# Attention weighing in a one-core transformer step: values stationary in two column halves, four heads' probabilities moving, 1/den turned to feature-major

## The chip, the cores and the metric

The kernel runs on one core of a Trainium2 chip. The metric is the device time of one execution in microseconds (us). The core has TensorE (PE in the profile; its loads of the stationary operand are PEld), VectorE (DVE), ScalarE (ACT), GpSimd (POOL) and SyncE (SP); each works its own queue strictly in the order in which the program issues instructions, except that PE may load a stationary operand ahead. The whole program is written under a manual schedule: the order of the Python calls is the order in each queue.

## The reference, cut to what matters

Two trunk layers over 384 tokens (three tiles of 128: latent tiles 0 and 1, context tile 2) of 1024 features. Layer 0 is feed-forward, attention, feed-forward; layer 1 has a recurrent mixer in the middle. The change is in the attention:

```python
p = softmax_with_sink(s, sink)          # e / (sum(e) + exp(sink - m))
return jnp.einsum('bhgqk,bkhd->bqhgd', p, v)     # then @ w_attn_out
```

There are 16 query heads of 64 features and 4 key/value heads, so that four query heads (a quadruple) share one v. A latent tile of 128 queries sees three blocks of 128 keys, the context tile one block.

## The kernel before, in words

Weights stream from HBM through three raw buffers; each chunk of 512 KB is split by ACT (L195) and DVE (L196) into two parts of lower precision, and PE multiplies in three passes (`mm3`, L447 to L450). Beside this a planner spreads "units" of the modulation vectors (`pace`, L311; one unit is one DVE instruction on 1024 columns, L242 or L244, and every second unit needs a 512 KB load, L230) over calls of `pace` in each stage: `set_pace(n, calls)` says up to which unit and in how many calls.

The attention (`attention`, L745) has three stages: the projections to q, k and v (to L899); the core (L903 to L1028); and the output projection `project_out` (L465), whose stationary operand is `hT`, the feature-major attention output, in chunks of 128 features.

The core runs over 36 items: 16 heads of latent tile 0, four quadruples of context heads, 16 heads of latent tile 1. Iteration i of its loop issues, in this order:

- `expo(i + 1)` (L934, ACT): exponential of the scores with the sum along the row accumulated to `den`,
- `flip(i)` (L945): PE turns the probabilities, one 128x128 transpose for each key block (L950), and ACT copies them from PSUM to `pT` (L951),
- `score(i + 2)` (L913, PE): two matmuls (L920) and for latent items a mask matmul (L923), into one of three PSUM banks,
- `weigh(i - 1)` (L953, PE): for each head and key block one matmul (L960) with the turned probabilities stationary and the 64 columns of v moving; the result is token-major, 64 columns for each head,
- `top(i + 2)` and `shift(i + 2)` (L925, L929, DVE): row maximum and the bias for the exponential,
- `pace()`, and after items 3, 8, 13 and 18 a weight split.

When 8 heads are complete (a "half"), the events of `O_LAGS` (L34) are fired 0 to 5 iterations later: `o_prep` (exponential of the sink term), `o_norm` (DVE: add, reciprocal, and 512 columns times 1/den out of PSUM, L972 to L974), `o_turn` (four PE transposes to feature-major, L431), `o_hi` and `o_lo` (ACT and DVE write the two parts of `hT`, L435 and L440). The last half's events that lie behind the loop run inside `project_out` (`flush`, L1030). What an item hands on from engine to engine is PE score, DVE maximum and bias, ACT exponential, PE flip, ACT copy, PE weighing.

Of the kernel before, what the change touches and what calls it, by code (L numbers as in the profile page):

```python
# [33 lines left out]
O_LAGS = [(0, 1, 0), (2, 1, 1), (4, 0, 2), (4, 1, 3), (5, 1, 4)]  # L34
# [3 lines left out]
def hybrid_step_kernel(  # L38
# [103 lines left out]
    add_rows(w_attn_out[0])  # L142
# [23 lines left out]
    def w_dma():  # L166
        j = ws["dma"]
        if j < len(chunks):
            SP.dma_start(out=view_like(raw_of(j), chunks[j].shape), in_=chunks[j])
            ws["dma"] += 1  # L170
# [574 lines left out]
    def attention(pending, perm):  # L745
# [6 lines left out]
        set_pace(5.5, 9)  # L752
        aux[0] = None
        with ExitStack() as es:
# [9 lines left out]
            qs = pool.tile([P, NT, 16, 2, 64], F32, name="qs")  # L764
            k_sb = pool.tile([P, 4, 256], F32, name="k_sb")
            pb = [pool.tile([P, 512], F32, name=f"p{i}") for i in range(3)]
            pT = [pool.tile([P, 512], F32, name=f"pT{i}") for i in range(2)]
# [134 lines left out]
            oslot = {t: alloc() for t in range(2)}  # L902
# [42 lines left out]
            def flip(i):  # L945
# [5 lines left out]
                S.activation(out=pT[i % 2][:, 0:w * P], in_=tb[:, 0:w * P], func=AF.Copy)  # L951

            def weigh(i):  # L953
                t, h0, nh, n, k0 = shape(i)
                src = pT[i % 2]
                for a in range(nh):
                    h = h0 + a
                    for j in range(n):
                        o = (a * n + j) * P
# [5 lines left out]
            def o_prep(t, half):  # L965
                hs = slice(8 * half, 8 * half + 8)
# [3 lines left out]
            def o_norm(t, half, i):  # L970
                hs = slice(8 * half, 8 * half + 8)
                V.tensor_tensor(out=den[:, t, hs], in0=den[:, t, hs], in1=esk[:, hs], op=ALU.add)  # L972
                V.reciprocal(out=den[:, t, hs], in_=den[:, t, hs])
                V.tensor_tensor(  # L974
                    out=slots[oslot[i]][:, half * 512:half * 512 + 512].rearrange("p (h d) -> p h d", h=8),
                    in0=bank(6 + half).rearrange("p (h d) -> p h d", h=8),
                    in1=den[:, t, hs].unsqueeze(2).to_broadcast([P, 8, 64]), op=ALU.mult,
                )

            def o_turn(t, half, i):  # L980
                turn(slots[oslot[i]], t, (bank(5), bank(5)), (half,))
# [14 lines left out]
            events = {}  # L996
            nd = 0
            for i in range(n):
                t, h0, nh = items[i]
                if h0 + nh in (8, 16):  # L1000
                    half = (h0 + nh) // 8 - 1
                    for lag, step, fn in O_LAGS:
                        args = (t, half) if fn == 0 else (t, half, nd % 2)
                        events.setdefault((i + lag, step), []).append(((o_prep, o_norm, o_turn, o_hi, o_lo)[fn], args))
                    nd += half

# [4 lines left out]
            for i in range(n + 1):  # L1011
# [7 lines left out]
                if i > 0:  # L1019
                    weigh(i - 1)  # L1020
# [554 lines left out]
```

## Time and profile before

| | |
|---|---|
| median of 3 runs | 1604.59 us (1603.9 to 1604.62) |
| profiled execution | 1604.8 us, span 1603.0 us |
| PE busy in the span | 97% |
| core of the attention, first score to first matmul of the output projection | 383.21 to 447.20 us |

The span is the time from the first to the last instruction of the profiled execution; about 2 us of the execution lie around it. A busy PE is not PE at its peak, since matmuls overlap; how fast a stretch of PE work goes is read from the distance of starts.

### The profile page before, as it was taken

How to read it: one execution, taken by the hardware profiler on the slowest of the kernel's cores; microseconds unless marked ns; L12 is line 12 of the kernel's file. 1: busy time of each engine (PE TensorE's matmuls, PEld its weight loads, DVE VectorE, ACT ScalarE, POOL GpSimd, SP SyncE). 2: the span in 40 equal slices, each digit the busy share in tenths (PEclk: the TensorE clock that was granted, in tenths of full speed). 3: DMA queues.
4: the chain of work that ended last, by engine and by line, in shares of the span. 5: the costliest groups of instructions: out<-in, count | busy, mean ns of one | idle time of the engine just before them, and what ended most of it. 6: DMA issues, size and time to landing. Idle time of an engine off the chain costs nothing.

```text
span 1603.0 us, 22629 instructions
## 1 busy us (share of the span) xinstructions
PE 1556.7 (97%) x8846; PEld 1419.6 (89%) x8846; DVE 1050.1 (66%) x1385; ACT 659.4 (41%) x1123; POOL 162.4 (10%) x308
## 2 busy tenths in 40 slices
PE   6999999999999999999999999999999899999997
PEld 4899987887889999988999998889999789999885
DVE  3887788577747777885676788556665765444552
ACT  3432234465745223334423233456656444323341
POOL 1111111000010111120011111000000110000000
PEclk9999999999999999999999999999999999999999
DMA  8776767352125676674467667433233335544441
GB/s 304 248 248 213 223 216 238 100 158 69 64 93 172 210 216 217 200 241 140 135 209 215 206 211 247 147 119 109 85 112 88 110 108 167 158 147 130 148 141 40
DMA packets 164091, 264.50 MB, mean 165 GB/s; under 512 B 10432, under 2 KB 122144, under 8 KB 163984
## 3 DMA queue, kind: packets, MB, share of 16 engines
q1 hardware_dynamic: 140592, 187.27, 36.2%
q0 software_dynamic: 22864, 75.36, 15.4%
q8 instruction: 69, 1.13, 0.3%
q10 hardware_dynamic: 528, 0.43, 0.1%
q14 instruction: 38, 0.31, 0.1%
HBM read 260.01 MB, written 3.01 MB: 164 GB/s over the span
## 4 chain that ended last, share of the span: by engine, by line
PE 87%; DVE 6%; ACT 3%; issue 1%; DMA 1%; POOL 0%; DVEq 0%; POOLq 0%; ACTq 0%
PE pb L448 14%; PE pb L449 14%; PE pb L450 14%; PE pb L458 13%; PE pb L460 12%; PE pb L463 12%; DVE wl L196 1%; PE pb L960 1%; PE pb L269 1%; ACT wh L195 1%; PE pb L950 1%; PE pb L920 1%; DVE sig L1100 1%; DVE slot L244 1%; PE pb L1152 1%
## 5 line engine op out<-in xcount | busy, mean ns | idle before, releaser
L196 DVE TENSOR_TENSOR wl<-raw,wh 128x1024 fp32r<-128x1024 f32 x297 | 362.1, 1224 | 245.9 <-ACT wh L195 245.6
L195 ACT ACTIVATE wh<-raw 128x1024 fp32r<-128x1024 f32 x299 | 315.0, 1059 | 479.0 <-PE pb L463 319.4
L458 PE MATMUL pb<-hT,wh 128*128 128x384 f32 (+1 forms) x1248 | 411.1, 333 | 0.0
L460 PE MATMUL pb<-hT,wl 128*128 128x384 f32 (+1 forms) x1248 | 407.1, 330 | 0.0
L244 DVE SCALAR_TENSOR_TENSOR slot<-araw,sc,slot 128x1024 f32<-128x1024 f32 x224 | 282.3, 1279 | 0.0
L463 PE MATMUL pb<-hT,wh 128*128 128x384 f32 (+1 forms) x1248 | 260.4, 329 | 0.0
L458 PEld LDWEIGHTS pb<-hT,wh 128*128 128x128 f32 x1248 | 235.4, 189 | 6.2 <-issue 5.9
L460 PEld LDWEIGHTS pb<-hT,wl 128*128 128x128 f32 x1248 | 235.3, 189 | 0.2
L463 PEld LDWEIGHTS pb<-hT,wh 128*128 128x128 f32 x1248 | 216.4, 189 | 0.0
L448 PE MATMUL pb<-wh,gh 128*128 128x512 f32 x384 | 150.7, 393 | 0.2 <-DVE dump L279 0.2
L450 PE MATMUL pb<-wh,gl 128*128 128x512 f32 x384 | 149.5, 389 | 0.0
L449 PE MATMUL pb<-wl,gh 128*128 128x512 f32 x384 | 149.5, 389 | 0.0
L230 POOL DMA_DIRECT2D araw<-in_w_ada_dram x128 | 69.2, 541 | 689.6 <-DVE slot L244 574.2
L448 PE MATMUL pb<-hT,wh 128*128 128x384 f32 x352 | 119.6, 340 | 4.9 <-ACT hT L1451 4.9
L449 PE MATMUL pb<-hT,wh 128*128 128x384 f32 x352 | 119.0, 338 | 0.2 <-DVE hT L1455 0.2
L450 PE MATMUL pb<-hT,wl 128*128 128x384 f32 x352 | 118.4, 336 | 0.0
L448 PE MATMUL pb<-wh,hT 128*128 128x512 f32 (+1 forms) x258 | 93.7, 363 | 2.7 <-DVE slot L1310 1.9
L449 PE MATMUL pb<-wl,hT 128*128 128x512 f32 (+1 forms) x258 | 90.4, 350 | 0.8 <-DVE wl L196 0.8
L450 PE MATMUL pb<-wh,hT 128*128 128x512 f32 (+1 forms) x258 | 90.5, 351 | 0.0
L448 PEld LDWEIGHTS pb<-wh,gh 128*128 128x128 f32 x384 | 72.1, 188 | 19.4 <-issue 3.4
L450 PEld LDWEIGHTS pb<-wh,gl 128*128 128x128 f32 x384 | 72.1, 188 | 15.1
L449 PEld LDWEIGHTS pb<-wl,gh 128*128 128x128 f32 x384 | 72.1, 188 | 14.7
(236 smaller groups left out, 2069.1 us busy)
## 6 DMA issues: line engine op xcount, KB each, us to landing
raw<-in_w_ffn_in_dram SPq DMA_DIRECT2D x176, 512.0 KB, 4.5
araw<-in_w_ada_dram POOLq DMA_DIRECT2D x128, 512.0 KB, 4.5
raw<-in_w_ffn_out_dram SPq DMA_DIRECT2D x88, 512.0 KB, 4.0
raw<-in_w_rec_in_dram SPq DMA_DIRECT2D x40, 512.0 KB, 3.6
slot<-dsc POOLq DMA_DIRECT2D x24, 256.0 KB, 5.8
raw<-in_w_qkv_dram SPq DMA_DIRECT2D x12, 512.0 KB, 3.9
raw<-in_w_attn_out_dram SPq DMA_DIRECT2D x8, 512.0 KB, 3.3
raw<-in_w_rec_out_dram SPq DMA_DIRECT2D x8, 512.0 KB, 3.2
```

Of the source, the lines that this page charges most:

```text
L195: S.activation(out=h, in_=r, func=AF.Copy)
L196: ws["eng"].tensor_tensor(out=lo, in0=r, in1=h.bitcast(F32), op=ALU.subtract)
L230: G.dma_start(out=araw[j % NA], in_=w_ada[kd[0], (j % 8) * P:(j % 8 + 1) * P, acol(kd):acol(kd) + 1024])
L244: V.scalar_tensor_tensor(out=acc[v], in0=src, scalar=s_, in1=acc[v], op0=ALU.mult, op1=ALU.add)
L269: T.matmul(out=bank[32 * r:32 * r + 32, :], lhsT=ones, rhs=acc[v][:, 512 * h:512 * h + 512], start=True, stop=True, skip_group_check=True,)
L448: T.matmul(out=out, lhsT=a[0], rhs=b[0], start=start, stop=False, skip_group_check=True)
L449: T.matmul(out=out, lhsT=a[0], rhs=b[1], start=False, stop=False, skip_group_check=True)
L450: T.matmul(out=out, lhsT=a[1], rhs=b[0], start=False, stop=stop, skip_group_check=True)
L458: T.matmul(out=out, lhsT=a[0], rhs=b[0], start=start, stop=False, skip_group_check=True)
L460: T.matmul(out=out, lhsT=x, rhs=y, start=False, stop=False, skip_group_check=True)
L463: T.matmul(out=out, lhsT=x, rhs=y, start=False, stop=stop, skip_group_check=True)
L920: T.matmul(out=ps[:, a, :], lhsT=hv[:, t, h, :], rhs=rhs, start=s == 0, stop=s == 1 and t == 2, skip_group_check=True)
```

## The change: what it does

`weigh` no longer runs for each item. It runs once for each group of 8 heads (two quadruples, one iteration after the group's last item), with v stationary: 64 columns of v for one quadruple write the upper 64 partitions of a PSUM bank, those of the other quadruple the lower 64, and the moving operand is the four heads' turned probabilities, 4 x 128 = 512 columns. So 112 matmuls of 64 columns become 28 of 512, in groups of 6 (latent tiles) or 2 (context). The output is feature-major at once, with another order of the heads along the features, so the rows of `w_attn_out` are loaded in that order, two DMAs of 64 partitions for a chunk in place of one of 128.

Since the queries now lie along the columns, 1/den has to be feature-major too: DVE spreads it to `rd` (two copies of 256 columns), PE turns `rd` (four transposes), ACT copies the result to a slot, DVE multiplies it by the PSUM bank of the weighing, and ACT and DVE write the two parts of `hT` from the slot. `pT` now keeps the turned probabilities of whole groups, in the space of the finished `qs`; the copy out of PSUM goes to DVE for items with i % 5 in (1, 3), 14 of 36, and to ACT for the others. `pace()` leaves the core's loop; the 8 units that stood there are done in the first feed-forward stage (5.5 in place of 5 for its `set_pace`), and the projection stage does units 88 to 95 in place of 80 to 87.

```diff
-O_LAGS = [(0, 1, 0), (2, 1, 1), (4, 0, 2), (4, 1, 3), (5, 1, 4)]
...
-    add_rows(w_attn_out[0])
+    for k in range(KD):
+        heads = [8 * (k // 4) + 4 * q + k % 4 for q in range(2)]
+        chunks.append(tuple(w_attn_out[0, 64 * h:64 * h + 64, :] for h in heads))
...
+            if isinstance(c_, tuple):
+                for q in range(2):
+                    SP.dma_start(out=raw_of(j)[64 * q:64 * q + 64, :], in_=c_[q])
...
-        set_pace(5.5, 9)
+        set_pace(6, 9)
...
-                S.activation(out=pT[i % 2][:, 0:w * P], in_=tb[:, 0:w * P], func=AF.Copy)
-
-            def weigh(i):
...
+                if i % 5 in (1, 3):
+                    V.tensor_copy(out=dst, in_=src)
+                else:
+                    S.activation(out=dst, in_=src, func=AF.Copy)
+
+            def weigh(t, gp, c):
+                n, k0 = (3, 0) if t < 2 else (1, 3)
+                for j in range(n):
+                    for q in range(2):
                         T.matmul(
-                            out=bank(6 + h // 8)[:, (h % 8) * 64:(h % 8) * 64 + 64], lhsT=src[:, o:o + P],
-                            rhs=v_sb[:, k0 + j, (h // 4) * 64:(h // 4) * 64 + 64], start=j == 0, stop=j == n - 1,
+                            out=bank(6 + c % 2)[64 * q:64 * q + 64, :], lhsT=v_sb[:, k0 + j, (2 * gp + q) * 64:(2 * gp + q) * 64 + 64],
+                            rhs=pT[c % 2][:, 4 * q:4 * q + 4, j, :], start=j == 0, stop=j == n - 1, skip_group_check=True,
                         )
...
+            def o_den(t, gp, c):
+                hs = slice(8 * gp, 8 * gp + 8)
                 V.tensor_tensor(out=den[:, t, hs], in0=den[:, t, hs], in1=esk[:, hs], op=ALU.add)
                 V.reciprocal(out=den[:, t, hs], in_=den[:, t, hs])
+                dv = den[:, t, hs].rearrange("p (q a) -> p a q", q=2)
+                for q in range(2):
+                    V.tensor_copy(out=rd[:, :, q, :], in_=dv[:, :, q:q + 1].to_broadcast([P, 4, 64]))
+
+            def o_row(t, gp, c):
+                for a in range(4):
+                    T.transpose(bank(5)[:, a * P:(a + 1) * P], rd[:, a].rearrange("p q d -> p (q d)"), ident)
+
+            def o_mul(t, gp, c):
+                u = half_of(slots[oslot], c % 2)
+                S.activation(out=u, in_=bank(5), func=AF.Copy)
+                V.tensor_tensor(out=u, in0=u, in1=bank(6 + c % 2), op=ALU.mult)
...
-            set_pace(6, 30)
...
+                    for lag, step, fn in ((0, 1, o_prep), (1, 0, weigh), (1, 1, o_den), (2, 0, o_row), (2, 1, o_mul), (3, 0, o_hi), (3, 1, o_lo)):
...
-                if i > 0:
-                    weigh(i - 1)
...
-                pace()
...
-        done = ffn(0, 0, 5, None, [0, 1, 2, 3], between)
+        done = ffn(0, 0, 5.5, None, [0, 1, 2, 3], between)
```

Around the end of the first 8 heads PE's queue stands like this before the change (`p` are the probabilities, `cf` holds the identity for a transpose, `pb_70` and `pb_71` are the banks of the output; items 8 and 9 flipped, 10 and 11 scored, 7 and 8 weighed):

```order
L950 MATMUL pb_67<-cf,p_2398 128x128 x3
L920 MATMUL pb_65<-kT,hT 128x384 x2
L923 LDWEIGHTS eye
L923 MATMUL pb_65<-hide_2405,eye 128x128
L960 MATMUL pb_70<-v_sb,pT_2400 128x64 x3
L950 MATMUL pb_68<-cf,p_2396 128x128 x3
L920 MATMUL pb_66<-kT,hT 128x384 x2
L923 LDWEIGHTS eye
L923 MATMUL pb_66<-hide_2405,eye 128x128
L960 MATMUL pb_71<-v_sb,pT_2399 128x64 x3
```

and like this after it (`qs` is now the space of the turned probabilities, `rd` the spread 1/den):

```order
L958 MATMUL pb_67<-cf,p_2411 128x128 x3
L928 MATMUL pb_65<-kT,hT 128x384 x2
L931 LDWEIGHTS eye
L931 MATMUL pb_65<-hide_2416,eye 128x128
L970 MATMUL pb_70<-qs,v_sb 64x512 x6
L958 MATMUL pb_68<-cf,p_2409 128x128 x3
L928 MATMUL pb_66<-kT,hT 128x384 x2
L931 LDWEIGHTS eye
L931 MATMUL pb_66<-hide_2416,eye 128x128
L990 MATMUL pb_69<-cf,rd 128x128 x4
L958 MATMUL pb_67<-cf,p_2410 128x128 x3
```

The three matmuls of one item between each score and the next flip have become six for eight items, in one piece behind the score of item 10 and ahead of the flip of item 9.

DVE's queue at the same place before the change, from the maximum of item 10 on:

```order
L927 TENSOR_REDUCE mx_2402<-pb_65 128x1
L932 SCALAR_TENSOR_TENSOR nm<-mx_2402,nsink 128x1
L927 TENSOR_REDUCE mx_2403<-pb_66 128x1
L932 SCALAR_TENSOR_TENSOR nm<-mx_2403,nsink 128x1
L972 TENSOR_TENSOR den<-den,esk 128x8
L973 RECIPROCAL den<-den 128x8
L974 TENSOR_TENSOR slot_110<-pb_70,den 128x512
L927 TENSOR_REDUCE mx_2401<-pb_64 128x1
L932 SCALAR_TENSOR_TENSOR nm<-mx_2401,nsink 128x1
L927 TENSOR_REDUCE mx_2402<-pb_65 128x1
```

and after it, from just behind the maximum of item 10:

```order
L982 TENSOR_TENSOR den<-den,esk 128x8
L983 RECIPROCAL den<-den 128x8
L986 COPY rd<-den 128x4x64 x2
L935 TENSOR_REDUCE mx_2414<-pb_66 128x1
L940 SCALAR_TENSOR_TENSOR nm<-mx_2414,nsink 128x1
L995 TENSOR_TENSOR slot_110<-slot_110,pb_70 128x512
L935 TENSOR_REDUCE mx_2412<-pb_64 128x1
L940 SCALAR_TENSOR_TENSOR nm<-mx_2412,nsink 128x1
L1003 TENSOR_TENSOR hT<-slot_110,hT 128x512
L962 COPY qs<-pb_68 128x384
L935 TENSOR_REDUCE mx_2413<-pb_65 128x1
```

The multiplication (L995), the low part of `hT` (L1003) and a copy of turned probabilities (L962) now stand between the maxima of items 11, 12 and 13.

## Rows read from the trace of the kernel before

**Rows 1.** The page, its part on busy time, share of the span and instructions of each engine.

```profile
PE 1556.7 (97%) x8846; PEld 1419.6 (89%) x8846; DVE 1050.1 (66%) x1385; ACT 659.4 (41%) x1123; POOL 162.4 (10%) x308
```

**Rows 2.** Busy time of each engine in stretches (us from the span's start, length, busy and count of PE, PEld, DVE, ACT, POOL, then the granted TensorE clock as a share of full speed, DMA share, GB/s): ten us of the first feed-forward stage, then the attention's projections, core and output projection.

```profile
240.00:250.00 10.00, 10.00 (x45) 8.28 (x45) 8.90 (x10) 4.25 (x6) 1.06 (x2) 1.00 0.76 248
341.00:383.20 42.20, 39.51 (x208) 32.76 (x206) 31.29 (x50) 21.34 (x39) 2.12 (x4) 1.00 0.48 157
383.20:447.20 64.00, 60.33 (x484) 52.47 (x484) 45.91 (x110) 46.34 (x146) 2.12 (x4) 1.00 0.14 45
447.20:500.00 52.80, 51.55 (x298) 43.89 (x298) 29.98 (x46) 26.23 (x52) 9.35 (x19) 1.00 0.35 111
```

**Rows 3.** Who waited for whom in the core, 383.2 to 447.2 us: engine, tile and line, what it waited for, us in total, times, longest.

```profile
PE pb L950 <- ACT p L940: 3.4, 4, 1.4
PE pb L920 <- ACT hT L883: 0.6, 1, 0.6
...
DVE mx L927 <- PE pb L923: 11.8, 15, 2.6
...
ACT p L940 <- DVE nm L932: 11.9, 16, 1.8
```

**Rows 4.** Timeline of PE's loads of the stationary operand in one steady round of the core (start, length): flip, score, mask, weighing, next flip.

```profile
404.56 0.37 PEld L950 LDWEIGHTS pb<-cf,p 128*128 128x128 f32 x3
404.90 0.30 PEld L920 LDWEIGHTS pb<-kT,hT 128*128 128x128 f32 x2
405.36 0.10 PEld L923 LDWEIGHTS <-eye 128*128 128x128 bf16 x1 [0.16 <-issue]
405.37 0.76 PEld L960 LDWEIGHTS pb<-v_sb,pT 128*128 128x128 f32 x6
405.99 0.20 PEld L950 LDWEIGHTS pb<-cf,p 128*128 128x128 f32 x1
```

**Rows 5.** Timeline of all engines at the start of the core, where nothing is weighed yet: flip of item 0, then item 2 from its score to its flip.

```profile
385.58 0.31 PEld L950 LDWEIGHTS pb<-cf,p 128*128 128x128 f32 x3 [1.33 <-ACT p L940]
...
385.86 0.30 PEld L920 LDWEIGHTS pb<-kT,hT 128*128 128x128 f32 x2
...
386.59 0.56 DVE L927 TENSOR_REDUCE mx<-pb 128x1 f32<-128x384 f32 x1 [1.16 <-PE pb L923]
...
387.18 0.16 DVE L932 SCALAR_TENSOR_TENSOR nm<-mx,nsink 128x1 f32<-128x1 f32 x1
...
387.43 0.58 ACT L940 ACTIVATE p<-pb,nm 128x384 f32<-128x384 f32 x1 [0.78 <-DVE nm L932]
...
388.16 0.20 PEld L950 LDWEIGHTS pb<-cf,p 128*128 128x128 f32 x2 [0.33 <-ACT p L940]
```

**Rows 6.** Timeline of PE's loads: the flips of items 15 (last of tile 0), 20 (first of tile 1) and 35 (last), and the first load of the output projection.

```profile
407.83 0.26 PEld L950 LDWEIGHTS pb<-cf,p 128*128 128x128 f32 x2
...
419.82 0.31 PEld L950 LDWEIGHTS pb<-cf,p 128*128 128x128 f32 x3
...
445.35 0.31 PEld L950 LDWEIGHTS pb<-cf,p 128*128 128x128 f32 x3
...
447.20 0.19 PEld L448 LDWEIGHTS pb<-wh,hT 128*128 128x128 f32 x1
```

**Rows 7.** Timeline of PE near the program's start: matmuls of 512 moving columns of f32 whose outputs lie on different strips of PSUM partitions (L1416: each makes two records of one pass; x4 is two matmuls), and what follows them.

```profile
15.93 1.03 PE L1416 MATMUL pb<-slot,sc 128*2 128x512 f32 x4
16.89 1.09 PE L431 MATMUL pb<-cf,slot 128*128 128x128 f32 x8
17.91 0.60 PE L1416 MATMUL pb<-slot,sc 128*2 128x512 f32 x2
...
18.34 0.60 PE L1416 MATMUL pb<-slot,sc 128*2 128x512 f32 x2
```

**Rows 8.** Groups of the core by line and shape, 383.2 to 447.2 us: count, busy us, mean ns of one, idle before them and its releaser.

```profile
L960 PE MATMUL pb<-v_sb,pT 128*128 128x64 f32 x224 | 30.6, 274 | 0.0
...
L951 ACT ACTIVATE pT<-pb 128x384 f32<-128x384 f32 x32 | 15.6, 487 | 0.3 <-PE pb L950 0.3
...
L244 DVE SCALAR_TENSOR_TENSOR slot<-araw,sc,slot 128x1024 f32<-128x1024 f32 x8 | 10.2, 1278 | 0.0
...
L940 ACT ACTIVATE p<-pb,nm 128x128 f32<-128x128 f32 x16 | 5.6, 371 | 1.2 <-DVE nm L932 1.2
...
L974 DVE TENSOR_TENSOR slot<-pb,den 128x512 f32<-128x512 f32 x5 | 3.5, 692 | 0.2
...
L951 ACT ACTIVATE pT<-pb 128x512 f32<-128x512 f32 x4 | 2.5, 619 | 0.0
```

**Rows 9.** Groups of the whole program by line and shape: the nearest instructions to the added ones.

```profile
L1471 DVE COPY slot<-pb 128x512 f32<-128x512 f32 x4 | 2.7, 684 | 0.7 <-PE pb L431 0.7
...
L653 DVE COPY g_early<-pb 128x256 f32<-128x256 f32 x3 | 1.3, 423 | 0.2 <-PE pb L652 0.2
```

**Rows 10.** Timeline: PE after an idle stretch near the program's start (the bracket is the idle time before), and the same shape some us later.

```profile
27.42 0.69 PE L448 MATMUL pb<-hT,wh 128*128 128x384 f32 x1 [3.16 <-ACT hT L1451]
...
31.13 0.52 PE L449 MATMUL pb<-hT,wh 128*128 128x384 f32 x1
...
32.77 0.33 PE L449 MATMUL pb<-hT,wh 128*128 128x384 f32 x1
```

**Rows 11.** Timeline: a weight split in the output projection of the attention.

```profile
453.17 1.06 ACT L195 ACTIVATE eh<-raw 128x1024 fp32r<-128x1024 f32 x1 [2.71 <-DMA raw<-in_w_attn_out_dram]
```

More of the change, by code (lines that the diff above doesn't have):

```diff
@@ L168, in w_dma @@
         if j < len(chunks):
-            SP.dma_start(out=view_like(raw_of(j), chunks[j].shape), in_=chunks[j])
+            c_ = chunks[j]
+            if isinstance(c_, tuple):
+                for q in range(2):
+                    SP.dma_start(out=raw_of(j)[64 * q:64 * q + 64, :], in_=c_[q])
+            else:
+                SP.dma_start(out=view_like(raw_of(j), c_.shape), in_=c_)
             ws["dma"] += 1
@@ L763, in attention @@
             small.tile([P, 16], F32, name="pad_a")
-            qs = pool.tile([P, NT, 16, 2, 64], F32, name="qs")
+            rd = small.tile([P, 4, 2, 64], F32, name="rd")
+            qf = pool.tile([P, NT * 16 * 2 * 64], F32, name="qs")
+            qs = qf.rearrange("p (t h s d) -> p t h s d", t=NT, h=16, s=2)
             k_sb = pool.tile([P, 4, 256], F32, name="k_sb")
             pb = [pool.tile([P, 512], F32, name=f"p{i}") for i in range(3)]
-            pT = [pool.tile([P, 512], F32, name=f"pT{i}") for i in range(2)]
             mxs = [pool.tile([P, 4], F32, name=f"mx{i}") for i in range(3)]
@@ L901, in attention @@
                 release(i)
-            oslot = {t: alloc() for t in range(2)}
+            oslot = alloc()
+            pT = [a.rearrange("p (h j n) -> p h j n", h=8, j=3) for a in (qf[:, 0:3072], qf[:, 3072:6144])]
             items = [(0, h, 1) for h in range(16)] + [(2, 4 * q, 4) for q in range(4)] + [(1, h, 1) for h in range(16)]
@@ L950, in flip @@
                     T.transpose(tb[:, j * P:(j + 1) * P], pb[i % 3][:, j * P:(j + 1) * P], ident)
-                S.activation(out=pT[i % 2][:, 0:w * P], in_=tb[:, 0:w * P], func=AF.Copy)
-            def weigh(i):
[L954 to L959, printed above, removed]
+                dst = pT[turns[i] % 2][:, h0 % 8:h0 % 8 + nh, 0:n, :]
@@ L967, in o_prep @@
+            def o_prep(t, gp, c):
+                hs = slice(8 * gp, 8 * gp + 8)
                 V.tensor_tensor(out=esk[:, hs], in0=nm[:, t, hs], in1=sink[:, hs], op=ALU.add)
                 S.activation(out=esk[:, hs], in_=esk[:, hs], func=AF.Exp)
-            def o_norm(t, half, i):
-                hs = slice(8 * half, 8 * half + 8)
+            def o_den(t, gp, c):
+                hs = slice(8 * gp, 8 * gp + 8)
                 V.tensor_tensor(out=den[:, t, hs], in0=den[:, t, hs], in1=esk[:, hs], op=ALU.add)
@@ L973, in o_norm @@
                 V.reciprocal(out=den[:, t, hs], in_=den[:, t, hs])
[L974 to L981, printed above, removed]
@@ new lines, in attention @@
+            n = len(items)
+            events = {}
+            nd, turns = 0, []
+            for i in range(n):
+                t, h0, nh = items[i]
+                turns.append(nd)
+                if h0 + nh in (8, 16):
+                    args = (t, (h0 + nh) // 8 - 1, nd)
+                    for lag, step, fn in ((0, 1, o_prep), (1, 0, weigh), (1, 1, o_den), (2, 0, o_row), (2, 1, o_mul), (3, 0, o_hi), (3, 1, o_lo)):
+                        events.setdefault((i + lag, step), []).append((fn, args))
+                    nd += 1
@@ L995, in attention @@
             expo(0)
[L996 to L1005, printed above, removed]
             def fire(i, step):
@@ L1032, in flush @@
                     fire(*key)
-                for i in oslot.values():
-                    release(i)
+                release(oslot)
             inner.close()
```

15 lines of the change are left out of this document (8 added, 7 removed).

## The prediction

> **What bounds the kernel now.** I read the page's busy times first: PE is busy in 97% of the span [rows 1], so time can only be won where PE's own work shrinks or where PE waits. Second, the table by stretches: only the attention's core is touched in its order, 64.0 us from the first score to the first matmul of the output projection; PE is busy for 60.3 of them, DVE for 45.9, ACT for 46.3, at full clock [rows 2]. Third, the waits of that stretch. PE waits 4.0 us in all, but on the other side ACT's exponential waits 11.9 us for DVE's bias in 16 of its turns, and DVE's maximum 11.8 us for PE's mask matmul in 15 [rows 3]. So PE looks like the bound, but the items' hand-over from engine to engine is close behind it. How close is the question that decides this change, and the timeline answers it twice.
>
> A steady round of PE's queue takes 405.99 - 404.56 = 1.43 us for one item: flip 0.34, score and mask 0.47, weighing 0.62 [rows 4]. At the start of the core nothing is weighed yet, and there one sees the hand-over alone: score of item 2 at 385.86, its maximum at 386.59, bias at 387.18, exponential at 387.43, flip at 388.16. That is 2.30 us from an item's score to its flip; the score of item i+2 stands right behind the flip of item i (385.58 to 385.86, 0.28 us; 0.34 in the steady round). So flip to flip of two items can't be shorter than 2.58 to 2.64 us, 1.31 us for one item [rows 4, 5]. PE's queue exceeds that by only 0.12 us. Taking the weighing out of the round frees 0.62 us of PE, of which 0.12 us is worth something; the other 0.50 us become idle time of PE.
>
> **The change part by part.** All terms are for the core, held against its own 64.0 us: 2.4 to the first flip (383.2 to 385.58), 22.25 to the flip of item 15, 11.99 to that of item 20, 25.53 to that of item 35, 1.85 to the output projection [rows 2, 5, 6].
>
> *The piece of weighing.* No row shows a 64-column half of the array. The nearest are matmuls whose outputs lie on different strips of partitions: two of them, two passes each with 512 columns of f32, are through after 16.89 - 15.93 = 0.96 us, and passes start 0.43 us apart (17.91, 18.34) [rows 7]. Two passes are 0.86, so two such matmuls ran side by side, and 0.10 went to the change over. Six matmuls are then 3 x 0.86 + 0.2 = 2.8 us, two are 1.06. Bounds: without the change over 2.6 and 0.86; one half after the other 5.4 and 1.9. I take 2.8 and 1.06, by the nearest row. The Trainium skill, "TensorEngine Tiling (Array Packing)", section "Key Properties", states that changing the tiling mode drains TensorE; the 0.10 us agrees, and with no drain the four long pieces of a core would be 0.8 us shorter in all. The piece stands in PE's queue ahead of the next flip, as the order shows; it uses up the 0.50 us that PE would idle, and the rest, 2.3 us (0.56 for two matmuls), delays both items that are on their way, since neither has slack to catch up with.
>
> *Behind the piece.* Queued behind the normalising are the maxima of the next items. From the flip of item 9 at 0: score of 11 to 0.81, four transposes to 1.23, ACT's copy to about 2.0 (0.62 for 512 columns, a hand-over of some 0.1 each side), DVE's multiplication 2.1 to 2.8 (0.69, as the old one [rows 8]). The maximum of item 12 was due at 2.3 (flip of 10 at 1.23, score 0.34 later, 0.73 to the maximum): 0.5 late. ACT's high part takes until 3.6, DVE's low part until 4.4, the copy of item 11 until 4.95; the maximum of item 13 was due at 3.7: 1.25 late. PE takes flips in order, so the later one counts nearly in full: 1.2 us for a group, from 0 (all of it absorbed) to 1.75 (both added).
>
> *Copies on DVE.* 14 copies leave ACT, which had room (0.49 each [rows 8]), for DVE. A copy of 384 columns lies between 0.42 (256) and 0.68 (512 columns) [rows 9]: 0.55. It ends at flip + 0.6 + 0.55, while the next maximum is due at flip + 0.34 + 0.73: 0.1 late. For 12 such items, half of them noticed because two items alternate: 0.6 us; between 0 and 1.2.
>
> *The sum.* Tile 0: 15 x 1.31 + 2.3 + 1.2 = 23.15, for 22.25: +0.9. Item 15 to 20: the context items are paced by ACT, four exponentials 0.35 apart (0.37 each [rows 8]) and a copy of 512 columns, some 1.9; 5 x 1.9 + 2.3 + 0.56 + 1.2 = 13.55, for 11.99: +1.6. Tile 1: 15 x 1.31 + 2.3 + 0.56 + 3 x 1.2 = 26.1, for 25.53: +0.6. End: the last flip, its copy and the whole piece, 0.6 + 0.5 + 2.8 = 3.9, for 1.85, where the old weighing of the last item but one already ran beside the copy: +2.05. With the copies +0.6 this is +5.75 us. In these terms the old kernel's own disturbances are already gone: the 8 units (10.2 us of DVE [rows 8]) and the old transposes of the output sit in its segments, not in 1.31.
>
> *What costs nothing.* The 8 units go to the first feed-forward stage, 10.2 us of DVE spread over its whole length. DVE is busy for 8.9 of 10 us in its densest part [rows 2]; with 1.76 units for a call in place of 1.6 that becomes 9.4, and the split weights are made four chunks ahead of PE. Cover: PE's own 10.0 of 10. If it is gone in the densest 30 us, up to 2 us. The projections' two first units get 0.5 us longer (L244 for L242), in a stretch where DVE is busy for 31.3 of 42.2 us [rows 2]: 0, at most 1. Two DMAs of 64 partitions for one of 128: SP has only loads to issue, and the one place where a split waits for such a load is ACT's 2.71 us in the output projection [rows 11], in a stretch where PE is busy for 51.55 of 52.8 us [rows 2]; 0, at most 1 us if both halves land later. The spreading of 1/den (two DVE copies, under 0.42 each) stands beside the piece on PE.
>
> The execution shown took 1604.8; 1604.8 + 5.75 = 1610.55. The median of the runs is 0.2 below that execution: **1610.4**.
>
> **The rivals.** *PE's queue was the bound (faster).* All of the saving counts: weighing 32 x 0.62 + 16 x 0.21 = 23.2 us becomes 4 x 2.8 + 2 x 1.06 = 13.3, a gain of 9.9: 1595. For it: PE's 60.3 busy us of 64.0 and only 4.0 us of waits [rows 2, 3]. Against it: the hand-over of 2.58 us for two items in a place without any weighing [rows 5]. It decides from the point where an item gets from score to flip in less than about 1.3 us, so that PE's 0.81 us of flip and score set the round. The Trainium skill, "TensorEngine Tiling (Array Packing)", section "When to Use Tiling", recommends just this exchange of stationary and streaming operand with two column tiles where the moving side has 64 columns; by that rule the weighing is halved, and the row of strips agrees, but a rule for PE says nothing of a loop that waits for DVE and ACT.
>
> *A wash.* After a piece two flips stand close together, and items then travel in pairs; PE's hole behind a pair is 2.64 - 1.62 = 1.0 us, so a piece that falls into it costs 1.8, and a delayed maximum of one item hides behind the other. Three pieces at 1.8 and 0.5 for 1.2 behind five groups give 5.75 - 1.5 - 3.5 = +0.75: 1605.4. For it: DVE has 18 idle us in the core [rows 2]. Against: the piece's place, before the flip that is due.
>
> *The halves run one after the other*, so that the change doesn't do what it says: + 4 x 2.58 + 2 x 0.86 = 12 more, 1622. The rows of strips speak against it [rows 7]. Here belongs the clock: after 3.16 us of idle PE the matmuls of 384 columns took 0.52, later 0.33 [rows 10], which is the lower of the two levels, 1.2 GHz in place of 2.4. PE's share in the core falls, but no single wait in my layout reaches 2 us.
>
> **How the numbers follow.** Forecast 0.60, with its own range 1607.8 to 1614.5 (behind a group 0.7 to 1.75, copies 0 to 1.2, the hidden parts up to 2). PE as bound 0.13, wash 0.20, halves in turn or lower clock 0.07. The range 1598 to 1616 leaves out the last one, most of the first rival and a little of the forecast. About 0.2%, 3.2 us, is what a measurement can tell from no change; so slower means above 1607.8. The forecast gives 0.57 of it and the halves 0.07: slower 0.64. The wash with the forecast's lower end: 0.22. Faster 0.14.
>
> **What will show it.** In the changed profile: flips 1.3 us apart where nothing is weighed, if the hand-over binds, 0.8 to 1.0 if PE does; the six matmuls as one piece of 2.6 to 2.8 us, twice that if the halves take turns; PE's waits for the exponential in the core up from 3.4 to more than 15 us; DVE's maximum waiting less for PE; the core 68 to 73 us long; the first feed-forward stage as long as before. The prediction is wrong if the core is shorter than 64 us, or if time appears in the first feed-forward stage or in the output projection.

## The result and the profile after

The changed kernel is slower: 1613.32 us median (1610.51 to 1615.71), beside 1604.24 us (1602.74 to 1604.62) for the kernel before on the same chip; ratio 1.0054, 95% interval 1.0040 to 1.0068. The profiled execution took 1612.96 us, 8.2 more than that of before (1604.8): the core of the attention is 9.1 us longer, the first score comes 1.45 us earlier (383.22 to 381.77), and the rest behind the core differs by 0.4 us (1155.8 us to the end of the span before, 1156.2 now). Each kernel below has one profiled execution, from which its segments and its clock are read; its ratio comes from all its executions.

Busy time of the engines over the span, on the page of the changed kernel, for [rows 1]:

```profile
PE 1552.1 (96%) x8678; PEld 1401.9 (87%) x8678; DVE 1058.8 (66%) x1411; ACT 658.1 (41%) x1115; POOL 162.3 (10%) x308
```

Busy time in stretches, columns as in [rows 2]: the first feed-forward stage, the projections, the core, the output projection, and then pieces of the core.

```profile
240.00:250.00 10.00, 10.00 (x45) 6.88 (x44) 10.00 (x11) 3.55 (x5) 2.79 (x5) 1.00 0.80 256
341.00:381.80 40.80, 38.09 (x203) 31.60 (x201) 31.11 (x49) 19.91 (x37) 2.12 (x4) 1.00 0.48 142
381.80:454.90 73.10, 56.59 (x317) 35.58 (x317) 46.30 (x128) 44.18 (x137) 0.00 (x0) 0.93 0.05 15
454.90:508.00 53.10, 51.86 (x300) 44.22 (x300) 30.39 (x47) 27.22 (x54) 9.33 (x19) 1.00 0.36 110
...
384.20:395.40 11.20, 8.24 (x54) 5.90 (x54) 7.28 (x21) 7.71 (x23) 0.00 (x0) 1.00 0.00 1
...
421.40:428.70 7.30, 4.40 (x29) 2.71 (x27) 5.73 (x16) 4.03 (x12) 0.00 (x0) 1.00 0.25 75
428.70:433.00 4.30, 2.68 (x17) 1.93 (x17) 3.16 (x9) 3.01 (x9) 0.00 (x0) 0.98 0.00 0
433.00:436.50 3.50, 3.33 (x14) 2.43 (x13) 1.99 (x5) 1.92 (x8) 0.00 (x0) 0.53 0.00 0
...
441.20:446.30 5.10, 3.02 (x22) 2.15 (x20) 4.38 (x11) 3.43 (x11) 0.00 (x0) 1.00 0.00 0
446.30:449.50 3.20, 2.18 (x9) 1.47 (x9) 1.44 (x4) 1.64 (x6) 0.00 (x0) 0.53 0.00 0
449.50:452.00 2.50, 2.49 (x7) 1.39 (x9) 0.86 (x4) 0.93 (x3) 0.00 (x0) 0.50 0.00 0
```

PE is busy for 3.7 us less in the core than before (56.59 for 60.33, though part of it now ran at half the clock) and the core is 9.1 us longer: PE is no longer what it waits for. The last column but two is the new thing: the granted clock, 1.00 all through the old core, is at half (1.2 GHz in place of 2.4) from about 433 to 436.5 and from 446.5 into the last piece. Ahead of the first fall PE was busy for 4.40 of 7.30 and 2.68 of 4.30 us, ahead of the second for 3.02 of 5.10; in the first stretch, where nothing is weighed yet and the clock stayed, for 8.24 of 11.20.

Who waited for whom in that core, for [rows 3]:

```profile
PE pb L958 <- ACT p L948: 13.6, 23, 1.2
PE pb L990 <- DVE rd L986: 2.8, 2, 1.5
...
ACT p L948 <- DVE nm L940: 12.5, 14, 1.6
...
DVE mx L935 <- PE pb L931: 12.1, 11, 2.6
DVE mx L935 <- PE pb L928: 2.8, 3, 2.4
```

PE waits for the exponential 13.6 us for 3.4. The second row is new: the turning of 1/den waits for its spreading (L986) in two groups.

Timeline of PE's loads, for [rows 4 and 6]: flips of items 0, 7, 8, 9 with the first piece of weighing between 8 and 9, the waiting row of 1/den, and the end with the last flip, its piece, and the output projection.

```profile
384.13 0.31 PEld L958 LDWEIGHTS pb<-cf,p 128*128 128x128 f32 x3 [1.33 <-ACT p L948]
...
393.09 0.31 PEld L958 LDWEIGHTS pb<-cf,p 128*128 128x128 f32 x3 [0.35 <-ACT p L948]
...
394.62 0.31 PEld L958 LDWEIGHTS pb<-cf,p 128*128 128x128 f32 x3 [0.70 <-ACT p L948]
...
395.51 0.20 PEld L970 LDWEIGHTS pb<-qs,v_sb 128*64 128x64 f32 x4
396.00 0.14 PEld L970 LDWEIGHTS pb<-qs,v_sb 128*64 128x64 f32 x2 [0.29 <-issue]
396.42 0.14 PEld L970 LDWEIGHTS pb<-qs,v_sb 128*64 128x64 f32 x2 [0.29 <-issue]
...
398.24 0.31 PEld L958 LDWEIGHTS pb<-cf,p 128*128 128x128 f32 x3 [0.81 <-issue]
...
421.01 0.42 PEld L990 LDWEIGHTS pb<-cf,rd 128*128 128x128 f32 x4 [1.47 <-DVE rd L986]
...
449.51 0.50 PEld L958 LDWEIGHTS pb<-cf,p 128*128 128x128 f32 x3 [1.39 <-ACT p L948]
...
450.99 0.49 PEld L970 LDWEIGHTS pb<-qs,v_sb 128*64 128x64 f32 x3 [0.36 <-ACT qs L964]
451.90 0.44 PEld L970 LDWEIGHTS pb<-qs,v_sb 128*64 128x64 f32 x2 [0.42 <-issue]
452.75 0.44 PEld L970 LDWEIGHTS pb<-qs,v_sb 128*64 128x64 f32 x2 [0.42 <-issue]
...
454.86 0.19 PEld L454 LDWEIGHTS pb<-wh,hT 128*128 128x128 f32 x1 [0.81 <-issue]
```

The first piece: two loads (one for each column half) every 0.43 us, so the halves do run side by side, 395.51 to the next flip at 398.24, 2.73 us. The last piece: the same pairs 0.85 to 0.91 us apart, at the lower clock, 450.34 to 454.86.

The core by segments, in all kernels (first score to first flip is 2.36 throughout; starts are those of the flips' first matmuls, up to 0.12 from the loads of [rows 6]; "half clock" is the time in the core, in us, at half the granted clock):

| kernel | tile 0 | context | tile 1 | end | core | half clock | ratio to before, interval |
|---|---|---|---|---|---|---|---|
| before | 22.37 | 11.87 | 25.54 | 1.88 | 64.0 | 0 | |
| forecast | 23.15 | 13.55 | 26.1 | 3.9 | 69.75 with copies | 0 | |
| changed | 22.94 | 14.43 | 28.01 | 5.35 | 73.1 | 10.2 | 1.0054 (1.0040 to 1.0068) |
| e1_units | 21.94 | 11.66 | 24.34 | 1.88 | 62.2 | 0 | 0.9992 (0.9982 to 1.0001) |
| e2_thin | 20.78 | 15.73 | 23.27 | 1.44 | 63.6 | 10.2 | 1.0005 (0.9995 to 1.0015) |
| e3_warm | 23.74 | 15.03 | 27.20 | 3.84 | 72.2 | 0 | 1.0067 (1.0055 to 1.0079) |
| e4_den | 23.03 | 17.94 | 25.83 | 5.10 | 74.3 | 10.2 | 1.0062 (1.0042 to 1.0081) |
| e12_warmden | 23.83 | 15.01 | 26.55 | 3.85 | 71.6 | 0 | 1.0052 (1.0036 to 1.0067) |
| e6_spread | 22.43 | 16.74 | 27.24 | 3.36 | 72.1 | 17.0 | 1.0104 (1.0087 to 1.0121) |
| e7_copies | 22.75 | 18.33 | 26.57 | 3.84 | 73.9 | 10.2 | 1.0064 (1.0051 to 1.0077) |
| e5_look3 | 18.49 | 12.83 | 23.48 | 3.85 | 61.0 | 3.4 | 1.0003 (0.9995 to 1.0012) |
| e8_both | 18.56 | 13.34 | 22.98 | 3.00 | 60.2 | 5.6 | 1.0049 (1.0037 to 1.0061) |
| e10_old3 | 22.57 | 11.95 | 24.07 | 1.87 | 62.8 | 0 | 1.0004 (0.9994 to 1.0014) |
| e9_pool | 18.13 | 12.28 | 22.64 | 3.84 | 59.3 | 3.4 | 0.9978 (0.9969 to 0.9987) |
| e11_all | 18.58 | 12.58 | 21.27 | 5.17 | 60.0 | 3.4 | 0.9985 (0.9976 to 0.9995) |

### The profile page after: what moved, and what is told of

The parts are those of the page before. It is cut to its first block, busy times and chain, and to the rows that moved or that the text cites. A ratio compares the mean times of both kernels' runs of the same rounds, so it can differ in the third digit from the quotient of the medians.

```text
span 1611.1 us, 22302 instructions
## 1 busy us (share of the span) xinstructions
PE 1552.1 (96%) x8678; PEld 1401.9 (87%) x8678; DVE 1058.8 (66%) x1411; ACT 658.1 (41%) x1115; POOL 162.3 (10%) x308
## 4 chain that ended last, share of the span: by engine, by line
PE 86%; DVE 7%; ACT 4%; issue 1%; DMA 1%; POOL 0%; DVEq 0%; ACTq 0%; POOLq 0%
PE pb L454 14%; PE pb L455 14%; PE pb L456 14%; PE pb L464 12%; PE pb L469 12%; PE pb L466 12%; DVE wl L202 1%; PE pb L275 1%; ACT wh L201 1%; DVE sig L1110 1%; PE pb L970 1%; ACT p L948 1%; PE pb L1162 1%; PE pb L958 1%; PE pb L1426 1%
## 5 line engine op out<-in xcount | busy, mean ns | idle before, releaser
L454 PEld LDWEIGHTS pb<-wh,gh 128*128 128x128 f32 x384 | 72.1, 188 | 17.9 <-issue 3.4
L456 PEld LDWEIGHTS pb<-wh,gl 128*128 128x128 f32 x384 | 72.1, 188 | 15.2
L455 PEld LDWEIGHTS pb<-wl,gh 128*128 128x128 f32 x384 | 72.1, 188 | 14.7
```

What stands on the lines that cost most here:

```text
L454: T.matmul(out=out, lhsT=a[0], rhs=b[0], start=start, stop=False, skip_group_check=True)
L455: T.matmul(out=out, lhsT=a[0], rhs=b[1], start=False, stop=False, skip_group_check=True)
L456: T.matmul(out=out, lhsT=a[1], rhs=b[0], start=False, stop=stop, skip_group_check=True)
```

## The experiments

**Is it the hand-over or PE's queue?** Two edits of the kernel before.

```diff
 e1_units
-        done = ffn(0, 0, 5, None, [0, 1, 2, 3], between)
+        done = ffn(0, 0, 5.5, None, [0, 1, 2, 3], between)
...
-                pace()
```

> The kernel before with one edit: the units of the gate matrix (L244) leave the attention's core and are done in the first feed-forward stage, paced as in the changed kernel. Hand-over theory: DVE loses 10.2 us of work inside the core; where the loop is bound by what DVE hands on, the core gets 1 to 3 us shorter than 64.0, and the first feed-forward stage stays as long as before: ratio 0.998 to 1.000. PE theory (the queue of PE is the bound): the core stays within 0.5 us of 64.0, ratio 1.000. If the moved units cost time where they go, the ratio is above 1.001 and the first score comes later than 383.2 us.

Measured: the core is 62.2 us, 1.8 shorter; the flips where nothing else is in PE's queue are 1.42 to 1.43 apart (398.75, 400.17, 401.60 in its timeline), without a wait in between. So the units had cost the old core 1.8 us, and what was left there was PE's round. The first score came at 383.90, 356.2 us behind the first large matmul of the first feed-forward stage (355.8 before; 355.65 in the changed kernel): 10.2 us of DVE put into that stage cost 0 to 0.4 us. The ratio can't be told from 1.

```diff
 e2_thin
-                    for j in range(n):
+                    for j in range(1):
```

> The kernel before with two of the three key blocks of the weighing left out for the 32 items of tiles 0 and 1 (their part of the output is not computed). PE's round falls from 1.43 to about 1.0 us, and nothing else changes. Hand-over theory: two items still need 2.58 to 2.64 us from score to flip, so a round falls to 1.3 at best: the core gets at most 32 x 0.12 = 4 us shorter, 60 to 64 us, ratio 0.9975 to 1.000, and PE's waits for the exponential rise from 3.4 us to 10 or more. PE theory: the core gets 32 x 0.41 = 13 us shorter, 51 us, ratio 0.992. If the granted clock falls in the core because PE idles, part of even the 4 us is lost.

Measured, in stretches of its core:

```profile
383.30:406.50 23.20, 18.49 (x134) 14.61 (x134) 16.84 (x41) 17.53 (x51) 0.53 (x1) 1.00 0.10 31
...
412.00:419.00 7.00, 7.00 (x35) 6.69 (x35) 3.69 (x9) 5.17 (x22) 0.00 (x0) 0.50 0.08 33
```

The fall of PE's work by 0.41 us an item gave 1.6 us over the 15 items of tile 0, 0.11 each (0.12 by the hand-over, 0.41 by PE's queue). PE's waits for the exponential rose from 3.4 to 9.6 us. Then the context items met half the clock and took 3.9 us longer, which ate the gain. The hand-over theory holds, by tile 0, which had the full clock; and in the old order too, with less work on PE, the clock fell.

**What are the 3.3 us beyond the forecast?** The candidates were the clock and the wait for the spread 1/den.

```diff
 e3_warm
                 if i < n:
+                    if i > 1:
+                        T.matmul(out=bank(3 + i % 2)[:, 0:256], lhsT=ident, rhs=v_sb[:, 0, :], start=True, stop=True, ...)
                     flip(i)
```

> The changed kernel with one useless matmul of 256 columns f32 (about 0.24 us) ahead of each flip, in PE's idle time, into the bank that the flip overwrites; 34 of them, 8 us of PE more. Clock theory: the granted clock falls to 0.5 near 433 and from 446 on because PE idles in 30 to 40% of the stretches before; with the holes filled the clock stays at 1.0 to the end of the core, and the last piece takes 2.8 us in place of 4: the core gets 2 to 3 us shorter than 73, ratio to the kernel before about 1.0035. Rival: the falls do not hang on these holes; the core stays at 73 us or gets longer, as the useless matmuls are 8 us more of PE: ratio 1.0055 to 1.008.

Measured, again in stretches of the core:

```profile
382.70:423.80 41.10, 37.69 (x229) 25.28 (x230) 26.59 (x71) 27.16 (x89) 0.00 (x0) 1.00 0.05 14
423.80:451.00 27.20, 24.34 (x143) 15.66 (x141) 18.80 (x54) 16.04 (x47) 0.00 (x0) 1.00 0.08 20
451.00:454.80 3.80, 3.80 (x15) 1.64 (x15) 0.87 (x4) 0.90 (x3) 0.00 (x0) 1.00 0.00 0
```

With 9 us more busy time for PE the clock stays at 1.00 and the core is 0.9 us shorter. The end takes 3.84 us for 5.35, tile 1 27.20 for 28.01; tile 0 and the context, which had the full clock anyway, are 0.8 and 0.6 longer, the price of the useless matmuls. In the time this is no gain: 1.0067, not below 1.0054. So the falls do hang on PE's idle time, and the end's 1.5 us are theirs; filling with useless work doesn't pay. Tile 1's 0.8 us is what is left of a larger gain: if the useless matmuls cost there what they cost in tile 0, the falls had taken about 1.6 us of it.

```diff
 e4_den
-                    for lag, step, fn in ((0, 1, o_prep), (1, 0, weigh), (1, 1, o_den), ...
+                    for lag, step, fn in ((-1, 1, o_prep), (1, 0, weigh), (0, 1, o_den), ...
```

> The changed kernel with the sink's exponential one item earlier and 1/den and its spreading (about 0.9 us of DVE) one item earlier, ahead of the maximum that follows. Theory of the spread: PE waits 1.5 and 1.3 us at the turning of 1/den of two groups because the spreading is late; those waits go and the core gets 1.5 to 2.8 us shorter than 73, ratio about 1.004. Rival (DVE's queue): the 0.9 us stand ahead of another maximum in its place, so the delay only moves; the core stays within 1 us of 73, ratio 1.0055.

Who waited for whom on PE in its core:

```profile
PE pb L958 <- ACT p L948: 17.2, 24, 2.6
PE pb L928 <- ACT hT L890: 0.6, 1, 0.6
```

And a stretch of it, with the granted clock:

```profile
411.00:420.00 9.00, 8.38 (x28) 3.85 (x28) 3.33 (x12) 4.99 (x27) 0.00 (x0) 0.62 0.22 58
```

The 2.8 us of waiting for the spread are gone, and PE waits 3.6 us more for the exponential. But here the clock was at 0.62 from 411 to 420 us, in the context, and fell again in the last piece, so the core's 74.3 us decide nothing by themselves. The useless matmul and the earlier 1/den in one kernel (the two diffs above), at a steady clock, do:

> Both edits at once: the useless matmul ahead of each flip, which held the clock at 1.0 in the core, and 1/den one item earlier, whose own run was clouded by a stretch at the lower clock. To be compared segment by segment with the run of the useless matmuls alone (tile 0 23.74, context 15.03, tile 1 27.20, end 3.84, core 72.17 us). If PE's two waits for the spread of 1/den (2.8 us there) are a cost of their own, context and tile 1 get 1.2 to 2.8 us shorter together, core 69.5 to 71 us, ratio 1.005 to 1.006. If the delay only moves to the maximum behind it, the core stays within 0.6 us of 72.2, ratio 1.0055 to 1.008. If the clock falls all the same, the useless matmuls are not what held it.

Measured:

```profile
383.00:454.70 71.70, 66.28 (x385) 42.37 (x385) 45.93 (x128) 44.23 (x138) 0.00 (x0) 1.00 0.06 16
```

Clock 1.00 throughout, core 71.6 us, 0.6 below the run of the useless matmuls alone, all of it in tile 1; the context is as long as there (15.01 for 15.03). Of 2.8 us of wait 0.6 came back: most of the delay only moves, for PE's waits for the exponential rise from 3.4 us in that run to 5.2 here.

**The forecast's two smaller terms.**

```diff
 e7_copies
-                if i % 5 in (1, 3):
-                    V.tensor_copy(out=dst, in_=src)
-                else:
-                    S.activation(out=dst, in_=src, func=AF.Copy)
+                S.activation(out=dst, in_=src, func=AF.Copy)
```

> The changed kernel with all 36 copies of turned probabilities on ACT, as in the kernel before. The forecast put the 14 copies on DVE at +0.6 us (0 to 1.2): the core gets 0 to 1.2 us shorter than 73, ratio 1.0045 to 1.0055. Rival: ACT was the next bound, at 0.71 + 0.50 us for an item of 1.31; then it gets longer by 1 us or more, ratio above 1.006.

Measured: tile 0 22.75 us, 0.2 shorter. The context met the lower clock (0.53 from 412 to 419) and took 3.9 us longer, so the core grew by 0.8. For the copies themselves only tile 0 is a clean reading. It holds 6 of the 14 copies, about half of the 12 items for which the forecast put +0.6, so 0.3 was due there and 0.2 came: the size was about right as far as this shows.

```diff
 e6_spread
+                        if fn is weigh and t < 2:
+                            for j in range(3):
+                                events.setdefault((i + lag + j, step), []).append((fn, args + ((j,),)))
```

> The changed kernel with the piece of six matmuls cut in three pairs, one pair in each of the three rounds behind a group (the turning of 1/den and what follows two rounds later; the last two pairs of the last group fall into the output projection). Theory of the piece: each pair of 0.53 us fits into the 0.50 us that PE idles in a round, so of the 2.3 us of a piece 1.9 come back, three times, and about 2 us at the end: core 65 to 69 us, ratio 1.000 to 1.003; the clock stays at 1.0. Rival: the delay comes from DVE's queue behind a piece and not from the piece; then the core stays above 71 us, ratio 1.004 or more.

(Two groups meet in the bank of the turned 1/den here, so one of them is normalised with the other's values; the instructions are the same.) Flips from item 8 on come 1.91 us apart for three rounds: 396.85, 398.75, 400.66. The expectation had halved the pair; two passes are 0.86, and of the 1.91 seen 0.81 are flip and score and 0.24 are left for the change over. That is 0.6 us over the hand-over's 1.31 in each round, 1.8 in all for 2.3, and tile 0 gained only 0.5; the other segments met half the clock and are no clean reading. The pairs of the last group, which fell into the output projection, made that stage 44.7 us long instead of 36.8; PE waited 3.3 us there for weight splits and ran 3.4 us at half the clock, the rest is not settled. Cutting the piece is no cure.

**Does a third item on its way lift the bound?** The scores of item i+3 in place of i+2 behind the flip of item i.

```diff
 e5_look3
-                ps = sview(i, bank(i % 3))
+                ps = sview(i, bank(i % 4))
...
-                    score(i + 2)
+                    score(i + 3)
...
-                            out=bank(6 + c % 2)[64 * q:64 * q + 64, :], ...
+                            out=bank(6)[64 * q:64 * q + 64, :], ...
```

> The changed kernel with the scores computed three items ahead instead of two (a fourth score bank, for which the weighing gives up its second output bank). Hand-over theory: three items instead of two share the 2.60 us from score to flip, so flips come 0.9 to 1.05 us apart where nothing is weighed, up to what ACT needs for one item (0.71 for exponential and read-out, 0.50 for six of ten copies); the core falls from 73 to 62 to 67 us, ratio 0.996 to 1.001. Rival: what an item takes of DVE and ACT binds, not the way through them; flips stay 1.2 to 1.3 apart and the core is above 70 us, ratio above 1.004.

Its timeline of loads, flips of items 3 to 8:

```profile
387.86 0.31 PEld L958 LDWEIGHTS pb<-cf,p 128*128 128x128 f32 x3
...
388.96 0.31 PEld L958 LDWEIGHTS pb<-cf,p 128*128 128x128 f32 x3 [0.27 <-ACT p L948]
...
389.72 0.31 PEld L958 LDWEIGHTS pb<-cf,p 128*128 128x128 f32 x3
...
390.75 0.31 PEld L958 LDWEIGHTS pb<-cf,p 128*128 128x128 f32 x3 [0.20 <-ACT p L948]
...
391.69 0.31 PEld L958 LDWEIGHTS pb<-cf,p 128*128 128x128 f32 x3
...
392.44 0.31 PEld L958 LDWEIGHTS pb<-cf,p 128*128 128x128 f32 x3
```

The first eight items take 7.24 us, 0.91 each, where they took 10.48, 1.31 each: the way through the engines was the bound, not what they do. The core falls by 12.1 us to 61.0, below the old one. Not all of it is the third item's: tile 0, at full clock in both, is 4.5 us shorter, but the end's 1.5 us and part of tile 1's 4.5 come from 3.4 us at half the clock in place of 10.2. In the time some 8 us of these came back (ratio 1.0003 for 1.0054). The two profiled executions differ by 9.1 us; there the first score came 1.1 us later than in the changed kernel (382.89 for 381.77) and the recurrent layer's stage took 1.9 us longer (266.5 for 264.6, see the last section). The control is the old order with the same look-ahead:

```diff
 e10_old3 (e1_units, and)
-                tb = bank(3 + i % 2)
+                tb = bank(4)
...
-                    score(i + 2)
+                    score(i + 3)
```

> Control: the kernel before with the units moved out of the core (62.2 us of core) and with the scores three items ahead (turned probabilities in one bank instead of two). Theory: with the weighing in the round, PE's 1.42 us are the bound and the deeper look-ahead has nothing to shorten: core 61 to 62.5 us, flips still 1.42 apart, ratio 0.998 to 1.000. Rival: the hand-over binds the kernel before too; then it gains as the changed kernel did, core below 58 us, ratio below 0.997. If the single bank for the turned probabilities is too few, flips get further apart than 1.42.

Core 62.8 us for 62.2, flips 1.42 to 1.43 apart as without it, ratio 1.0004: with the weighing in the round PE's queue is the bound, and a third item shortens no steady round. The control is not quite clean, since it has one bank for the turned probabilities where e5_look3 has two. Who waited for whom on PE in its core:

```profile
PE pb L950 <- ACT pT L951: 3.2, 4, 1.4
```

These 3.2 us of waiting for that bank, all but 0.2 of them between 412 and 423 us, around the context items, are a cost of the control alone; what the third item would win there with two banks was not tried.

**A version that beats both.**

```diff
 e8_both (e5_look3 and the cut of e6_spread, but)
+                        parts = ((0,), (1, 2)) if nd == 1 else ((0,), (1,), (2,))
```

> The changed kernel with both: scores three items ahead and the piece cut in pairs (second group of tile 0 in one pair and one of four matmuls). If the two causes are separate, the core falls to 59 to 62 us, below the 64.0 us of the kernel before: ratio 0.996 to 0.999. If the deeper look-ahead already absorbs the pieces, it equals the run with look-ahead alone within 1 us.

e8_both is e5_look3 with cut pieces. Tile 0 is as long as with the look-ahead alone, at full clock in both (18.56 for 18.49), and so nearly is tile 1, with 3.4 us at half the clock in both (22.98 for 23.48), so the look-ahead absorbs the pieces; the cut last piece again made the output projection long (45.2 us), which is about what 1.0049 has over 1.0003.

```diff
 e9_pool (e5_look3, and)
-                V.tensor_tensor(out=hT[:, t, 1, ks, :], in0=u, ...
+                G.tensor_tensor(out=hT[:, t, 1, ks, :], in0=u, ...
```

> The changed kernel with scores three items ahead (as in the run before with 61.0 us of core) and the five low parts (0.69 us of DVE each) on GpSimd. If, with the deeper look-ahead, what is left behind a piece is DVE's own work (1.28 us an item behind the pieces, 0.91 ahead of them), DVE loses 3.5 us, and the core gets 1.5 to 3.5 us shorter than 61.0; ratio 0.997 to 1.000. Rival: the pieces' 2.7 us of PE and ACT's copies set that pace; the core stays within 1 us of 61.0, ratio 0.9995 to 1.0012.

Core 59.3 us, 1.8 shorter again, and the time is below both kernels: 1601.35 us median beside 1605.67, ratio 0.9978, interval 0.9969 to 0.9987. On GpSimd a low part takes 1.27 us for DVE's 0.69, and GpSimd has next to nothing else to do there. Against e1_units, the old order without its units, the gain is not clear of noise: the intervals, 0.9969 to 0.9987 and 0.9982 to 1.0001, overlap. The old order with its low parts on GpSimd was not run.

```profile
L1003 POOL TENSOR_TENSOR hT<-slot,hT 128x512 fp32r<-128x512 f32 x5 | 6.3, 1268 | 55.2 <-ACT hT L999 55.2
```

```diff
 e11_all (e9_pool, and)
+                        parts = {0: ((0,), (1,), (2,)), 1: ((0,), (1, 2)), 4: ((0,), (1,), (2,))}.get(nd, ((0, 1, 2),))
```

> The same as the run with the low parts on GpSimd, and with the pieces of the first, second and fifth group cut in pairs over successive rounds, the last group's piece left whole. If a piece of 2.7 us still delays flips with three items ahead, the core gets 1 to 3 us shorter than that run; if the look-ahead already absorbs it, it stays within 1 us. Ratio 0.996 to 1.000.

e11_all leaves the last piece whole and cuts the others. Tile 0, at full clock in both, is 0.45 us longer (18.58 for 18.13): nothing is won by cutting. Tile 1 gained 1.4 us and the end lost 1.3, but the 3.4 us at half the clock lay in tile 1 in e9_pool and at the end here; within the error of the time it is e9_pool.

## Why the forecast was right in sign and 3.3 us short

**Right.** The hand-over: 1.31 us an item in the stretch without weighing, 10.48 / 8, as read from [rows 5]; PE's freed time was worth 0.11 us an item. The piece: 2.73 us for 2.8, and the flips around it 3.62 apart, 1.31 + 2.31 for 2.3. Behind the piece: 22.94 - 15 x 1.31 - 2.31 = 0.98 us for 1.2, and in the order forecast, as DVE's timeline behind the first piece shows: multiplication, maximum, low part, copy, and the maximum of item 13 at 402.85, 0.9 us behind its due 398.24 + 3.7.

```profile
400.31 0.69 DVE L995 TENSOR_TENSOR slot<-slot,pb 128x512 f32<-128x512 f32 x1 [0.32 <-ACT slot L994]
400.92 0.55 DVE L935 TENSOR_REDUCE mx<-pb 128x1 f32<-128x384 f32 x1
...
401.78 0.69 DVE L1003 TENSOR_TENSOR hT<-slot,hT 128x512 fp32r<-128x512 f32 x1
402.39 0.55 DVE L962 COPY qs<-pb 128x384 f32<-128x384 f32 x1
402.85 0.55 DVE L935 TENSOR_REDUCE mx<-pb 128x1 f32<-128x384 f32 x1
```

The end at full clock: 3.84 or 3.85 in five runs, for 3.9. The first feed-forward stage and the projections: 355.65 us for 355.8, so the moved units and the longer first units were hidden, though DVE was busy for 10.00 of 10 us in its densest part and not for 9.4. The split loads cost nothing that the output projection shows (36.8 us before and after). Luck: the 1.45 us by which the first score came early lie ahead of all this (the first large matmul at 26.12 for 27.42 [rows 10], with the same wait of 3.16 or 3.17 us; the other kernels, with the same code there, start it at 26.8 to 27.9), and they brought the time that much nearer to the forecast.

**Mis-sized.** The context: 14.43 us for 13.55 at full clock. The step "The spreading of 1/den (two DVE copies, under 0.42 each) stands beside the piece on PE" fails where the piece is only two matmuls: PE waited 1.3 and 1.5 us for it behind the two context groups. But e12_warmden shows these waits to be worth 0.6 us in the whole core, all of it in tile 1, and nothing in the context. What made the context 0.9 us longer is not shown; DVE's queue behind three groups in five items is a guess. The copies: of the +0.6 half was due in tile 0, and 0.2 was seen.

**Wrong.** "PE's share in the core falls, but no single wait in my layout reaches 2 us", with which the lower clock was put among the 7%. No wait reached 2 us (the longest of PE for the spread was 1.5, for the exponential 1.2), and the clock fell twice. At full clock tile 1 is 25.83 in e4_den, which lacks the waits for the spread (0.65 us there, by e12_warmden against e3_warm), so about 26.5 with them, for 26.1; here it was 28.01. So the clock took about 1.5 us there, as the useless matmuls also gave, and 1.5 at the end: 3.0 us, which is nearly the 3.3 between 9.1 and 5.75 (the context's +0.9 and tile 1's +0.4 against tile 0's -0.2 and the copies' -0.6, which the segments already hold, leave +0.3 with the smaller ones). Without it the core would have been 2.36 + 22.94 + 14.43 + 26.5 + 3.85 = 70.1, for 69.75 forecast; that the errors in the context, tile 1 and the copies nearly cancel is luck too. The executions without a profile point the same way: two show the profiled one's mean granted clock of 0.991 and took 1613.67 and 1615.71 us, one shows 0.994 and took 1610.51. That is one execution, and where its clock fell is not known.

**The signs named ahead.** The core, 73.1 us, is just over the 68 to 73 named. PE's wait for the exponential rose to 13.6 us, not above 15; with that for the spread it is 16.4. DVE's maximum did not wait less for PE (12.1 for 11.8): while PE does a piece no score is made. The wash, in which a piece costs only 1.8 us, was not seen: the flips around the pieces inside tile 0 and tile 1 are 3.62 and 3.63 us apart (436.51 to 440.14 the second), 2.3 over 1.31 each time. The rival "PE's queue was the bound" falls for this kernel, by e2_thin and by 1.31. Near its turning point it came into its own: in e5_look3 an item's share of the way was 2.6 / 3 = 0.87 us, flips came 0.91 us apart, near PE's 0.81, and the saved PE time showed. The Trainium skill, "TensorEngine Tiling (Array Packing)", section "When to Use Tiling", recommends the swap with two column tiles where the moving side has 64 columns. Here the halves did run side by side (passes 0.43 us apart), but the swap alone gave 1.0054, with the deeper look-ahead 1.0003, and 0.9978 with the low parts on GpSimd as well.

## What to carry to other kernels

Before moving work off a busy engine, find a stretch in which that work is absent and read the pace there: the difference of the two paces, not the work removed, is what the change can win. If the pace there is a way through several engines with two items on it, put a third item on the way together with the change: the core took 73.1 us with the change alone, 62.8 with the third item alone (and the units moved), 61.0 with both, 59.3 with the low parts moved too. And count TensorE's new idle time as a risk to its clock: here waits of at most 1.5 us each were followed by half the clock.

## What the runs showed that was not expected

The recurrent layer's stage, whose code no kernel here changes, took 262.8 to 268.9 us from profile to profile, by how often its clock fell. The whole stage, in the kernel before:

```profile
1051.70:1315.90 264.20, 251.40 (x1605) 234.77 (x1604) 163.48 (x289) 142.07 (x262) 12.68 (x20) 0.99 0.35 108
```

In e9_pool, with three falls (near 1073, 1195 and 1257 us):

```profile
1047.90:1316.80 268.90, 254.56 (x1606) 237.77 (x1605) 163.46 (x289) 142.13 (x263) 12.69 (x20) 0.98 0.35 106
...
1070.00:1076.00 6.00, 5.87 (x26) 5.87 (x27) 1.30 (x2) 4.11 (x9) 0.00 (x0) 0.72 0.30 88
1191.00:1199.00 8.00, 7.22 (x36) 6.99 (x36) 6.99 (x20) 2.43 (x9) 0.00 (x0) 0.79 0.46 131
1254.00:1260.00 6.00, 6.00 (x27) 5.32 (x28) 3.99 (x7) 0.62 (x2) 0.00 (x0) 0.72 0.29 87
```

In e12_warmden, with none:

```profile
1059.70:1322.50 262.80, 249.88 (x1606) 233.28 (x1605) 163.40 (x289) 142.16 (x263) 12.70 (x20) 1.00 0.36 109
```

These 6 us are as large as what was to be measured. They are probably most of the runs' spread: the executions of one kernel with the lower mean clock tend to be the longer ones (e12_warmden: 1618.19 and 1617.12 us at 0.992 and 0.993, 1610.31 to 1611.91 at 0.995 and 0.996; e9_pool: 1600.19 to 1605.74, its profiled execution the slowest and at 0.991, its lowest clock). So the core's length in the trace was the better measure of an edit, though it is one execution's. What decides how often the clock falls in that stage, and whether an edit in the core changes it, was not tried.
